# Second expert pass: activation loads on GpSimd's queue, gating in place, gate map built eight tokens at a time

## The chip, the cores and the metric

The kernel runs on one core of a Trainium2 chip. The metric is the time of one execution on the device in microseconds (us). Engines: TensorE (PE) multiplies matrices, VectorE (DVE) and ScalarE (ACT) work elementwise, GpSimd (POOL) and SyncE (SP) do little more here than start transfers. Every engine runs its own list of instructions in order. A transfer (DMA) is started by an instruction on one engine's queue, waits there for what it depends on, and is then moved by the 16 DMA engines that all queues share.

## What is computed

Two transformer blocks on 256 tokens of width 1024, in fp32. The second block has two layers, and each ends in a layer of 16384 experts:

```python
def peer(h, w_q, sub_keys, u_emb, v_emb):
...
    q = jnp.einsum('td,dhk->thk', x_t, w_q).reshape(T, PEER_HEADS, 2, PEER_HALF)
    s = jnp.einsum('thpk,hpnk->thpn', q, sub_keys).astype(jnp.float32)
    sv, si = lax.top_k(s, K)
...
    fv, fpos = lax.top_k(cand, K)
...
    gate = jax.nn.softmax(fv, axis=-1)
    u = u_emb[eidx]
    v = v_emb[eidx]
    act = jax.nn.gelu(jnp.einsum('thkd,td->thk', u, x_t).astype(jnp.float32), approximate=False)
    return jnp.einsum('thk,thkd->td', (gate * act).astype(x_t.dtype), v)
```

Each token has 8 heads that choose 16 experts each; an expert has a row of `u` and a row of `v`.

## The kernel before

The kernel doesn't gather rows. It computes the activation of every token with every expert, multiplies it by a gate map G that is zero where an expert was not chosen, and multiplies the result by all of `v`. fp32 operands are split into a high and a low part (`wh`, `wl`), and a product is made of three matmuls: high times high, high times low, low times high. A weight tile of 1 MB is 128 x 2048 and is split in four 128x512 pieces by `split_w` (L302 on ScalarE makes `wh`, L303 on VectorE makes `wl`).

`peer(l)` (L1369 to 1694) runs once in each layer:

- **Queries.** Eight `feat2` blocks give the scores; the top 16 of each are found on VectorE. Before that, `xd` is stored to DRAM (L1374), the only transfer that goes through GpSimd's queue.
- **First expert pass** (L1595 to 1609): 64 blocks over `peer_u`, each with one weight tile, matmuls L370 and L373, gelu, and a store of 256 KB of activations to DRAM on ScalarE's queue (L1604). Between the matmuls a list of side work is run at a set pace (`tick`, `side`): the selection, and then the gate map, four tokens at a time. `onehots` (L1530) makes two one-hot tables and a weighted one, with VectorE operations L1534 to L1536; `onelow` (L1539) makes the low part, L1541; `build` (L1543) multiplies them in eight f16 matmuls (L1547, L1548), which ScalarE copies into G (128 x 128 x 256 fp32). There are 64 such groups in a layer.
- **Second expert pass** (L1629 to 1641): for each of 64 steps `n`, a weight tile of `peer_v` (L1635, SyncE's queue, three buffers `w`), the gated activations from `gated(n)`, and 24 matmuls 128x512 (L423) into four accumulators.

`gated(n)` (L1577) loads 256 KB of activations `ag` (L1580, SyncE's queue), multiplies by G into `wt` (L1582, VectorE), and splits `wt` in high (L1589, ScalarE) and low (L1590, VectorE). `ag` and `wt` are tiles of the tag `k2`, which has five buffers of 128x512 fp32 (`NK2 = 5`) for all temporaries of the kernel. A load can start when a buffer of the tag is free.

During the second pass of layer 0 the kernel also loads 52 tiles of 512 KB of `ada_w` (L482, SyncE's queue) into parts of G that are used up, and VectorE reduces each (L483). In layer 1 that work is absent. The scheduler of the language fixes the order of each engine's instructions when the program is built.

`diag` (L209), a helper of the first block and the mixers, scales an identity matrix and has a tag of its own, `dg`, with two buffers.

Of the kernel before, what the change touches and what calls it, by code (L numbers as in the profile page):

```python
# [8 lines left out]
F32 = mybir.dt.float32  # L9
F32R = mybir.dt.float32r  # L10
F16 = mybir.dt.float16
# [8 lines left out]
P = 128  # L20
S = 256
# [10 lines left out]
NK2 = 5  # L32
# [43 lines left out]
def body(tc, A, out, dbg=None, stop=None):  # L76
    nc = tc.nc
    es = ExitStack()

    def pool(name, bufs=1, space=None, stack=es):  # L80
        kw = {} if space is None else {"space": space}
        return stack.enter_context(tc.tile_pool(name=name, bufs=bufs, **kw))
# [14 lines left out]
    st = pool("stage", 2)  # L97
# [110 lines left out]

    def diag(r):  # L209

        d = st.tile([P, P], F32, name="dg", bufs=2)
        nc.vector.tensor_scalar(d, ident, r, None, op0=OP.mult)
        return d

# [315 lines left out]
    def row_of(i, r):  # L530

        pr = pmm.tile([P, 512], F32, name="mm")
        for t in range(2):
            nc.tensor.matmul(pr[:, t * P:(t + 1) * P], ones, diag(r[:, t:t + 1]), start=True, stop=True)
        nc.scalar.activation(rows_rms[:, i, :], pr[:, 0:S], AF.Copy)
# [404 lines left out]
    for t in range(2):  # L940
        nc.tensor.matmul(pr[:, t * P:(t + 1) * P], ones, diag(rf[:, t:t + 1]), start=True, stop=True)
# [46 lines left out]
    for t in range(2):  # L988
        a_, b_ = ssx[:, 2 * t:2 * t + 1], ssx[:, 2 * t + 1:2 * t + 2]
        e_, c_ = r2_[:, 2 * t:2 * t + 1], r2_[:, 2 * t + 1:2 * t + 2]  # L990
        nc.vector.tensor_scalar(e_, a_, b_, D * EPS, op0=OP.add, op1=OP.add)
        nc.vector.tensor_scalar(e_, e_, EPS, None, op0=OP.mult)
        inv_rms(c_, ssf[:, 2 * t:2 * t + 1], ssf[:, 2 * t + 1:2 * t + 2], e_)
        by0.append(diag(c_))
# [374 lines left out]
    def peer(l, x, by, xstack):  # L1369
# [10 lines left out]
        ip = pool("peeri", stack=ps0)  # L1380
# [48 lines left out]
        def add(cost, f, *a):  # L1429
            side.append((cost, lambda: f(*a)))  # L1430
# [68 lines left out]
        def select():  # L1499

            for t in range(2):
                add(0.75, pairs, t)
                for h in range(8):
                    add(0.65, top16, FV[:, t, h], FP[:, t, h], cand[:, t, h])
                add(0.5, tables, t)
                add(0.8, places, t)
            add(1.4, gates)
            for t in range(2):
                wc = [(w, c) for w in range(2) for c in range(0, 16, 4)]
                for n, (w, c) in enumerate(wc):  # L1510
                    add(0.78, terms, t, w, c)
                    if n:
                        add(0.0, entry, t, *wc[n - 1])
                add(0.0, entry, t, *wc[-1])
                add(0.6, slots, t)
# [4 lines left out]
        def over(w, t0):  # L1520


            return ijg[:, w, t0:t0 + 4, None, :].to_broadcast(four)

        def pairs_of(v):
            return v.rearrange("p t (j a) -> p t j a", a=2)
# [3 lines left out]
        def onehots(t0):  # L1530
            ab = st.tile([P, 2, 4, P], F16, name="k2", bufs=NK2)
            a, b = ab[:, 0], ab[:, 1]
            e = ip.tile([P, 4, P], F16, name="ohe", bufs=2)
            nc.vector.tensor_tensor(pairs_of(e), places2, over(1, t0), op=OP.is_equal)  # L1534
            nc.vector.tensor_tensor(pairs_of(a), places2, over(0, t0), op=OP.is_equal)
            nc.vector.tensor_mul(pairs_of(b), pairs_of(e), over(2, t0))  # L1536
            hot[t0] = a, b, e
# [28 lines left out]
        side.popleft()[1]()  # L1566
        select()
        add(0.0, gate_map)
        for t0 in range(0, S + 8, 4):
            if t0 < S:  # L1570
                add(1.0, onehots, t0)
            if 4 <= t0 < S + 4:
                add(0.35, onelow, t0 - 4)
            if t0 >= 8:
                add(0.0, build, t0 - 8)

        def gated(n):  # L1577

            ag = st.tile([P, 2, S], F32, name="k2", bufs=NK2)
            nc.sync.dma_start(ag.rearrange("p j t -> p (j t)"), actd[n])  # L1580
            wt = st.tile([P, 2, S], F32, name="k2", bufs=NK2)
            nc.vector.scalar_tensor_tensor(wt, ag, 1.0 / GATE, G[0][:, 2 * n:2 * n + 2, :], op0=OP.mult, op1=OP.mult)  # L1582
            if n:
                whl = q4.tile([P, 2, 2, S], F32R, name="q4")
                wh_, wl_ = whl[:, 0], whl[:, 1]
            else:
                wh_ = st.tile([P, 2, S], F32R, name="k2", bufs=NK2)
                wl_ = st.tile([P, 2, S], F32R, name="k2", bufs=NK2)
            nc.scalar.activation(wh_, wt, AF.Copy)  # L1589
            nc.vector.tensor_sub(wl_, wt, wh_.bitcast(F32))  # L1590
            return wh_, wl_


        actd = []
        pace["rate"] = sum(c for c, _ in side) / (4 * 56)  # L1595
        for g in range(64):
            def ev_act(acc):
                ag = st.tile([P, 2, S], F32, name="k2", bufs=NK2)
                if g < LATE:
                    both(ag, acc)  # L1600
                    acc = ag
                nc.scalar.activation(ag, acc, AF.Gelu)
                ad = dr.tile([P, 2 * S], F32, name=f"act{l}_{g}")
                nc.scalar.dma_start(ad, ag.rearrange("p j t -> p (j t)"))  # L1604
                actd.append(ad)
            (feat2 if g < LATE else feat)(hl, A["peer_u_2"], (l * 64 + g) * P * 2048, ev_act)
            if g == 61:
                side_done()
                first_w = gated(0)
# [19 lines left out]
        for n in range(64):  # L1629
# [4 lines left out]
            w = wp.tile([P, 2048], F32, name="w")  # L1634
            nc.sync.dma_start(w, dap(A["peer_v_2"], l * 16384 * 1024 + n * 2048, [[P * 1024, P], [1, 2048]]))  # L1635
            wh_, wl_ = first_w if n == 0 else gated(n)
            if n < 63:
                for i in range(2):
# [35 lines left out]
    if stop == "xm0":  # L1674
        b1.close(); es.close()
        return
    x, ss, xs_ = peer(0, x, by, b1)
    dump("xp0", x)
    if stop == "xp0":
# [4 lines left out]
    if stop == "xm1":  # L1684
        xs_.close(); es.close()
        return
    x, ss, xs_, frow = peer(1, x, by, xs_)
    r_ = nrm.tile([P, 2], F32, name="rx2")
    o = out.rearrange("(t p) d -> p t d", p=P)
# [144 lines left out]
```

## Time and profile before

| | us |
|---|---|
| runs shown | 2221.74, 2221.75, 2216.76 |
| median | 2221.74 |
| profiled execution | 2223.68 |
| its span | 2221.9 |
| first expert pass, layers 0 and 1 | 523.9 to 897, 1477.8 to 1862 |
| second expert pass, layers 0 and 1 | 907.5 to 1264.6, 1861.6 to 2205.5 |

In the second pass the matmuls of line 423 begin and end the stage; the times in the last row are the starts of the first and the last of them. The span runs from the first to the last instruction of the profiled execution; the rest of its time lies around it. The granted clock of TensorE was 1.00 of full in every stretch shown. In views of the trace, `L1582 DVE` is an instruction of line 1582 on VectorE, `k<-k,G` are the tiles it writes and reads, and `[0.49 <-DMA k<-act]` says that its engine had been idle for 0.49 us before it and what ended that.

### The profile page before, as it was taken

What the parts mean: (1) busy time and instruction counts of PE and PEld (TensorE: products, weight loads), DVE (VectorE), ACT (ScalarE), POOL (GpSimd) and SP (SyncE); (2) the same over time, 40 slices, a digit from 0 to 9 for tenths busy, and PEclk for the clock granted to TensorE, in tenths of its full rate; (3) what the DMA queues carried; (4) which work ended last, traced back from release to release, by engine and by line L of the source; (5) the groups of instructions that cost most, each with busy time, mean ns of one, the idle gap of its engine ahead of it and who ended that gap; (6) DMA issues with size and microseconds to landing.
All of it is one profiled execution on the core that took longest, in us unless ns stands there. A gap on an engine that the chain in (4) does not pass through costs nothing.

```text
span 2221.9 us, 36167 instructions
## 1 busy us (share of the span) xinstructions
PE 2183.6 (98%) x12792; PEld 1865.7 (84%) x12792; DVE 1826.7 (82%) x4379; ACT 1326.6 (60%) x2448; POOL 21.2 (1%) x28
## 2 busy tenths in 40 slices
PE   8999999999999999999999999999999999999998
PEld 7889998888888888878777787888888888888886
DVE  7778888689988887688888888899888876777776
ACT  7656555555666666555555566566666666555554
POOL 0000000000000000000000010000000000000000
PEclk9999999999999999999999999999999999999999
DMA  6246787445655555889999643456555557666663
GB/s 244 96 167 256 271 303 281 160 173 206 226 212 207 198 212 209 283 314 332 323 321 322 215 157 122 171 193 239 203 201 210 196 212 259 250 248 245 244 240 143
DMA packets 107286, 503.30 MB, mean 227 GB/s; under 512 B 12513, under 2 KB 13665, under 8 KB 61794
## 3 DMA queue, kind: packets, MB, share of 16 engines
q1 hardware_dynamic: 87954, 465.19, 58.4%
q10 hardware_dynamic: 18864, 33.72, 4.1%
q8 instruction: 100, 1.64, 0.3%
q0 software_dynamic: 288, 2.10, 0.2%
q14 instruction: 80, 0.66, 0.1%
HBM read 464.25 MB, written 36.70 MB: 225 GB/s over the span
## 4 chain that ended last, share of the span: by engine, by line
PE 84%; DVE 7%; DMA 6%; ACT 1%; issue 1%; SPq 0%; DVEq 0%; ACTq 0%
PE acc L373 24%; PE acc L423 22%; PE acc L370 12%; DMA k<-act 6%; PE acc L308 4%; PE acc L311 4%; PE acc L312 4%; DVE wl L303 3%; PE acc L320 3%; PE acc L321 3%; PE acc L319 3%; PE mm L1547 1%; PE mm L1548 1%; DVE G L483 1%; PE pt L267 1%
## 5 line engine op out<-in xcount | busy, mean ns | idle before, releaser
L302 ACT ACTIVATE wh<-w 128x512 fp32r<-128x512 f32 (+1 forms) x1408 | 879.6, 630 | 652.6 <-PE acc L423 247.5
L303 DVE TENSOR_TENSOR wl<-w,wh 128x512 fp32r<-128x512 f32 (+1 forms) x1408 | 951.9, 689 | 205.7 <-ACT wh L302 198.2
L373 PE MATMUL acc<-q,wh 128*128 128x512 f32 x2240 | 797.3, 402 | 0.0
L423 PE MATMUL acc<-wh,q 128*128 128x512 f32 x1984 | 611.0, 390 | 0.0
L370 PE MATMUL acc<-q,wl 128*128 128x256 f32 x2240 | 584.3, 281 | 1.0 <-DVE wl L303 1.0
L373 PEld LDWEIGHTS acc<-q,wh 128*128 128x128 f32 x2240 | 408.1, 188 | 69.9
L370 PEld LDWEIGHTS acc<-q,wl 128*128 128x128 f32 x2240 | 422.6, 189 | 22.7 <-DVE wl L303 2.1
L423 PEld LDWEIGHTS acc<-wh,q 128*128 128x128 f32 x1984 | 372.4, 188 | 76.7
L423 PE MATMUL acc<-wl,q 128*128 128x512 f32 x992 | 387.4, 392 | 7.3 <-DVE wl L303 7.0
L423 PEld LDWEIGHTS acc<-wl,q 128*128 128x128 f32 x992 | 186.2, 188 | 52.7 <-DVE wl L303 14.5
L1582 DVE SCALAR_TENSOR_TENSOR k<-k,G 128x512 f32<-128x512 f32 x128 | 88.2, 690 | 65.9 <-DMA k<-act 65.0
L1410 ACT ACTIVATE k<-acc 128x512 f32<-128x512 f32 x124 | 74.0, 597 | 96.9 <-PE acc L373 96.8
L320 PE MATMUL acc<-q,wh 128*128 128x256 f32 x416 | 117.8, 284 | 0.5 <-DVE q L245 0.5
L319 PE MATMUL acc<-q,wh 128*128 128x256 f32 x416 | 117.3, 283 | 0.7 <-ACT q L244 0.7
L321 PE MATMUL acc<-q,wl 128*128 128x256 f32 x416 | 117.5, 283 | 0.0
L1411 DVE TENSOR_TENSOR k<-acc,k 128x512 f32<-128x512 f32 x124 | 85.0, 686 | 17.6 <-ACT k L1410 17.3
L311 PE MATMUL acc<-wl,q 128*128 128x512 f32 (+1 forms) x224 | 89.4, 400 | 0.0
L1590 DVE TENSOR_TENSOR q<-k,q 128x512 fp32r<-128x512 f32 x126 | 86.2, 684 | 0.8
L312 PE MATMUL acc<-wh,q 128*128 128x512 f32 (+1 forms) x224 | 86.6, 400 | 0.0
L308 PE MATMUL acc<-wh,q 128*128 128x512 f32 (+1 forms) x224 | 85.9, 402 | 0.4 <-ACT q L244 0.4
L1589 ACT ACTIVATE q<-k 128x512 fp32r<-128x512 f32 x126 | 77.8, 617 | 13.8 <-DVE k L1582 13.8
L320 PEld LDWEIGHTS acc<-q,wh 128*128 128x128 f32 x416 | 79.7, 192 | 0.8 <-DVE q L245 0.7
(459 smaller groups left out, 2660.4 us busy)
## 6 DMA issues: line engine op xcount, KB each, us to landing
w<-in_peer_u_dram SPq DMA_DIRECT2D x128, 1024.0 KB, 4.9
w<-in_peer_v_dram SPq DMA_DIRECT2D x128, 1024.0 KB, 5.3
act<-k ACTq DMA_DIRECT2D x128, 256.0 KB, 3.0
k<-act SPq DMA_DIRECT2D x128, 256.0 KB, 5.4
G<-in_ada_w_dram SPq DMA_DIRECT2D x52, 512.0 KB, 7.2
w<-in_w_gu_dram SPq DMA_DIRECT2D x22, 1024.0 KB, 4.8
adw<-in_ada_w_dram SPq DMA_DIRECT2D x44, 512.0 KB, 5.6
w<-in_peer_w_q_dram SPq DMA_DIRECT2D x16, 1024.0 KB, 4.9
```

The costliest lines, as they stand in the source:

```text
L302: ada_p["act"] = nc.scalar.activation(h[:, :n], src, AF.Copy).ins.name
L303: i_ = nc.vector.tensor_sub(l[:, :n], src, h[:, :n].bitcast(F32))
L308: i_ = nc.tensor.matmul(ps, lh, wh, start=start, stop=False)
L311: nc.tensor.matmul(ps, lh, wl, start=False, stop=False)
L312: i_ = nc.tensor.matmul(ps, ll, wh, start=False, stop=stop)
L319: nc.tensor.matmul(ps, wh, h, start=start, stop=False)
L320: nc.tensor.matmul(ps, wh, l, start=False, stop=False)
L321: nc.tensor.matmul(ps, wl, h, start=False, stop=stop)
L370: nc.tensor.matmul(to[:, 0, :], wl[:, ws], part(hl, k, 0), start=False, stop=False)
L373: nc.tensor.matmul(to.rearrange("p a s -> p (a s)"), wh[:, ws], hl[k // 2][:, k % 2].rearrange("p a s -> p (a s)"), start=k == 0, stop=k == 7)
L423: nc.tensor.matmul(ps[t, hf], lhs, ww[hf], start=first and lhs is h and ww is wh, stop=last and lhs is l)
L1582: nc.vector.scalar_tensor_tensor(wt, ag, 1.0 / GATE, G[0][:, 2 * n:2 * n + 2, :], op0=OP.mult, op1=OP.mult)
```

## The change

Four edits. The load of the activations moves from SyncE's queue to GpSimd's, and their product with G overwrites them, so that `gated` takes one buffer of `k2` where it took two. In the gate map, two groups of four tokens are built one right after the other, `onelow` follows its own `onehots`, and the tag `ohe` has three buffers. `diag` takes a buffer of `k2` where it had a tag of its own. Lines behind the edit move down by three: L1580, L1582, L1589, L1590 and L1635 are L1583, L1585, L1592, L1593 and L1638 after the change.

```diff
--- before.py
+++ after.py
@@ -208,7 +208,7 @@
 
     def diag(r):
 
-        d = st.tile([P, P], F32, name="dg", bufs=2)
+        d = st.tile([P, 512], F32, name="k2", bufs=NK2)[:, 0:P]
         nc.vector.tensor_scalar(d, ident, r, None, op0=OP.mult)
         return d
 
@@ -1530,7 +1530,7 @@
         def onehots(t0):
             ab = st.tile([P, 2, 4, P], F16, name="k2", bufs=NK2)
             a, b = ab[:, 0], ab[:, 1]
-            e = ip.tile([P, 4, P], F16, name="ohe", bufs=2)
+            e = ip.tile([P, 4, P], F16, name="ohe", bufs=3)
             nc.vector.tensor_tensor(pairs_of(e), places2, over(1, t0), op=OP.is_equal)
             nc.vector.tensor_tensor(pairs_of(a), places2, over(0, t0), op=OP.is_equal)
             nc.vector.tensor_mul(pairs_of(b), pairs_of(e), over(2, t0))
@@ -1566,19 +1566,22 @@
         side.popleft()[1]()
         select()
         add(0.0, gate_map)
+
         for t0 in range(0, S + 8, 4):
             if t0 < S:
                 add(1.0, onehots, t0)
-            if 4 <= t0 < S + 4:
-                add(0.35, onelow, t0 - 4)
-            if t0 >= 8:
+            if t0 >= 8 and t0 % 8 == 0:
                 add(0.0, build, t0 - 8)
+                add(0.0, build, t0 - 4)
+            if t0 < S:
+                add(0.35, onelow, t0)
 
         def gated(n):
 
             ag = st.tile([P, 2, S], F32, name="k2", bufs=NK2)
-            nc.sync.dma_start(ag.rearrange("p j t -> p (j t)"), actd[n])
-            wt = st.tile([P, 2, S], F32, name="k2", bufs=NK2)
+
+            nc.gpsimd.dma_start(ag.rearrange("p j t -> p (j t)"), actd[n])
+            wt = ag
             nc.vector.scalar_tensor_tensor(wt, ag, 1.0 / GATE, G[0][:, 2 * n:2 * n + 2, :], op0=OP.mult, op1=OP.mult)
             if n:
                 whl = q4.tile([P, 2, 2, S], F32R, name="q4")
```

The number of instructions stays the same on PE, DVE and ACT. The 128 loads of activations leave SyncE's list and stand in GpSimd's, in the order of `n`.

**VectorE in the second pass of layer 1.** `k_23128` and `k_23130` are one step's `ag` and `wt`, and the numbers of the next step are higher by 49. Before:

```order
L1590 TENSOR_TENSOR q_22936<-k_22934,q_22936 128x512
L1582 SCALAR_TENSOR_TENSOR k_23130<-k_23128,G 128x512
L303 TENSOR_TENSOR wl<-w,wh 128x512 x4
L1590 TENSOR_TENSOR q_22985<-k_22983,q_22985 128x512
L303 TENSOR_TENSOR wl<-w,wh 128x512
L1582 SCALAR_TENSOR_TENSOR k_23179<-k_23177,G 128x512
L303 TENSOR_TENSOR wl<-w,wh 128x512 x3
L1590 TENSOR_TENSOR q_23034<-k_23032,q_23034 128x512
```

After the change a step has one buffer, and numbers rise by 48:

```order
L1593 TENSOR_TENSOR q_22846<-k_22843,q_22846 128x512
L303 TENSOR_TENSOR wl<-w,wh 128x512 x3
L1585 SCALAR_TENSOR_TENSOR k_23083<-k_23083,G 128x512
L303 TENSOR_TENSOR wl<-w,wh 128x512
L1593 TENSOR_TENSOR q_22894<-k_22891,q_22894 128x512
L303 TENSOR_TENSOR wl<-w,wh 128x512 x3
L1585 SCALAR_TENSOR_TENSOR k_23131<-k_23131,G 128x512
L303 TENSOR_TENSOR wl<-w,wh 128x512
L1593 TENSOR_TENSOR q_22942<-k_22939,q_22942 128x512
```

Between `L1593` of a step and the multiplication five steps later, which takes the same buffer (`k_22843`, then `k_23083`), stand three `L303`, or two in every fourth step; right behind the multiplication come one or two `L303` and the next `L1593`.

**VectorE in the second pass of layer 0.** Before:

```order
L1582 SCALAR_TENSOR_TENSOR k_11902<-k_11900,G 128x512
L303 TENSOR_TENSOR wl<-w,wh 128x512
L1590 TENSOR_TENSOR q_11802<-k_11800,q_11802 128x512
L488 TENSOR_TENSOR mod<-mod,cols 128x8
L303 TENSOR_TENSOR wl<-w,wh 128x512 x3
L483 SCALAR_TENSOR_TENSOR G,mod<-G 128x1024
L1582 SCALAR_TENSOR_TENSOR k_11953<-k_11951,G 128x512
L303 TENSOR_TENSOR wl<-w,wh 128x512
```

After, with the numbers rising by 50 or 51 a step:

```order
L1593 TENSOR_TENSOR q_11837<-k_11834,q_11837 128x512
L1585 SCALAR_TENSOR_TENSOR k_12034<-k_12034,G 128x512
L303 TENSOR_TENSOR wl<-w,wh 128x512 x3
L483 SCALAR_TENSOR_TENSOR G,mod<-G 128x1024
L303 TENSOR_TENSOR wl<-w,wh 128x512
L1593 TENSOR_TENSOR q_11887<-k_11884,q_11887 128x512
L1585 SCALAR_TENSOR_TENSOR k_12085<-k_12085,G 128x512
```

Here the multiplication that takes the buffer of `k_11834` is that of `k_12085`; a whole step of VectorE's work stands between the `L1593` that frees the buffer and it.

## Rows read from the trace of the kernel before

**Rows 1.** Windows: length, busy us (and count) by engine, PE clock, DMA share, GB/s.

```profile
523.86:897.00 373.14, 372.65 (x2489) 320.31 (x2488) 322.70 (x832) 245.96 (x426) 0.00 (x0) 1.00 0.60 213
943.00:1247.00 304.00, 296.73 (x1290) 239.86 (x1289) 259.36 (x443) 164.78 (x270) 0.00 (x0) 1.00 0.89 318
1900.00:2202.00 302.00, 302.00 (x1338) 250.15 (x1337) 217.22 (x338) 168.05 (x276) 0.00 (x0) 1.00 0.66 238
```

**Rows 2.** The same for line 423 alone, both second expert passes.

```profile
907.50:1264.55 357.05, 349.77 (x1511) 281.45 (x1512) 1.00 0.86 308
1861.60:2205.50 343.90, 343.89 (x1511) 283.34 (x1512) 1.00 0.67 240
```

**Rows 3.** Waits (us, times, longest): 907 to 1262, 943 to 1247, 1900 to 2202.

```profile
PE acc L423 <- DVE wl L303: 7.0, 11, 1.1
...
DVE k L1582 <- DMA k<-act: 44.3, 42, 2.6
...
DVE k L1582 <- DMA k<-act: 14.0, 11, 3.1
```

**Rows 4.** DMA issues, count, KB, median us to landing: 943 to 1247, 1862 to 2200.

```profile
k<-act SPq DMA_DIRECT2D x54, 256.0 KB, 6.7
...
k<-act SPq DMA_DIRECT2D x62, 256.0 KB, 3.2
```

**Rows 5.** Timeline, layer 0: start, us, engine, line; VectorE, then SyncE's queue.

```profile
1030.74 0.69 DVE L1582 SCALAR_TENSOR_TENSOR k<-k,G 128x512 f32<-128x512 f32 x1 [1.33 <-DMA k<-act]
...
1034.90 0.68 DVE L1590 TENSOR_TENSOR q<-k,q 128x512 fp32r<-128x512 f32 x1
1035.74 0.69 DVE L1582 SCALAR_TENSOR_TENSOR k<-k,G 128x512 f32<-128x512 f32 x1 [0.15 <-DMA k<-act]
...
1041.08 0.69 DVE L1582 SCALAR_TENSOR_TENSOR k<-k,G 128x512 f32<-128x512 f32 x1 [0.49 <-DMA k<-act]
...
1035.62 0.36 SPq L1580 DMA_DIRECT2D k<-act  x1
```

**Rows 6.** Timeline, layer 1: VectorE, then SyncE's queue.

```profile
2005.31 0.69 DVE L1582 SCALAR_TENSOR_TENSOR k<-k,G 128x512 f32<-128x512 f32 x1
...
2010.78 0.69 DVE L303 TENSOR_TENSOR wl<-w,wh 128x512 fp32r<-128x512 f32 x1
2011.39 0.68 DVE L1582 SCALAR_TENSOR_TENSOR k<-k,G 128x512 f32<-128x512 f32 x1
...
2006.03 0.32 SPq L1580 DMA_DIRECT2D k<-act  x1
```

**Rows 7.** GpSimd's two transfers (line 1374), and SyncE's load of the same tensor.

```profile
L1374 POOL DMA_DIRECT2D xd<-xf x1: 702/702/702, 450.5 to 450.5; - x1
...
DMA to landing us min/median/max: 5.7/6.3/6.9
...
w<-xd SPq DMA_DIRECT2D x2, 1024.0 KB, 4.7
```

**Rows 8.** Timeline of TensorE around one build in layer 0's first pass.

```profile
699.73 0.28 PE L370 MATMUL acc<-q,wl 128*128 128x256 f32 x1
...
700.09 0.28 PE L370 MATMUL acc<-q,wl 128*128 128x256 f32 x1
700.21 0.23 PE L1547 MATMUL mm<-k 128*128 128x128 f16 x1
...
700.55 0.22 PE L1547 MATMUL mm<-k 128*128 128x128 f16 x1
...
700.95 0.28 PE L370 MATMUL acc<-q,wl 128*128 128x256 f32 x1
```

**Rows 9.** Groups of VectorE, 523.86 to 897: count, busy, mean ns, idle before.

```profile
L1534 DVE TENSOR_TENSOR ohe<-iota,ijg 128x512 f16<-128x512 f16 x64 | 27.1, 424 | 15.2 <-PE mm L1548 14.6
L1541 DVE TENSOR_TENSOR ohe<-ohe,ijg 128x512 f16<-128x512 f16 x64 | 26.9, 421 | 0.9
L1536 DVE TENSOR_TENSOR k<-ohe,ijg 128x512 f16<-128x512 f16 x64 | 26.7, 418 | 0.2
```

## The prediction

> **What bounds the kernel now.** I read the windows first, since a stage shows its limit there. In the first expert pass of layer 0 TensorE is busy for 372.65 of 373.14 us, and in the second pass of layer 1 for 302.00 of 302.00 us [rows 1]. Both are at TensorE's pace, and nothing that another engine does faster can shorten them. The second pass of layer 0 is the exception: 296.73 of 304.00 us, with the DMA engines at 0.89 and VectorE busy for 259.36 us [rows 1]. The two second passes do the same 1512 matmuls, and the windows of line 423 alone show 357.05 us for layer 0 and 343.90 us for layer 1 [rows 2]. So layer 0 loses 13.1 us, and the ideal step is 343.9 / 63 = 5.46 us, call it 5.45.
>
> Who is late there? The list of waits says that TensorE waited for `wl`, 7.0 us in 11 waits, and that VectorE, which makes `wl`, waited 44.3 us in 42 waits for the loads of activations [rows 3]. Those take 6.7 us from issue to landing in layer 0, and 3.2 us in layer 1 [rows 4]. The timeline shows one: it is issued at 1035.62, as L1590 of an earlier step has freed a buffer (1034.90 + 0.68), and the multiplication waits until 1041.08 [rows 5]. In layer 1 a load goes out at 2006.03, as the multiplication of 2005.31 ends, and the next multiplication is at 2011.39, behind other work [rows 6]: 5.36 us are there for a load of 3.2 us. That is the slack which layer 1 has and layer 0 hasn't.
>
> **The change, part by part.**
>
> *Layer 0, second pass.* Gating in place doesn't bring the loads forward by as much as two buffers saved would suggest: the scheduler runs the multiplication farther ahead, and all five buffers are held until `L1593` of a step has read them. The load of step n+5 leaves at the end of `L1593` of n. In the rows after the change, one step of VectorE's work stands between that instruction and the multiplication that needs the load. Follow the load, its multiplication, and VectorE's work up to the next but one `L1593`: that is one latency L, 0.04 us to issue (1035.62 against 1035.58, [rows 5]) and one step of work, 1030.74 to 1035.58 = 4.84 us [rows 5], for two steps. The step takes (L + 4.9) / 2, and TensorE's 5.45 us are met up to L = 6.0 us. What will L be? GpSimd's queue isn't shown with a load. Its two stores of 1 MB landed 5.7 and 6.9 us after issue; SyncE's loads of the same tensor took 4.7 us [rows 7]. So GpSimd's queue cost 1.0 to 2.2 us more. The least for L is layer 1's 3.2 + 1.0 = 4.2 us, and the stage then loses nothing (gain 13.1 us). The most is 6.7 + 2.2 = 8.9 us, a step of 6.9 us and a loss of some 1.45 x 50 steps = 73 us, less the 13.1 that are lost already: +59 us. I take L near the low end, since these loads no longer stand in a queue behind a weight tile and an `ada_w` tile; with the engines busy at 0.89 a little stays: **-10 us**.
>
> *Layer 1, second pass.* Here the new order costs. Between `L1593` of n and the multiplication of n+5 stand three `L303`, which come at TensorE's pace, and right behind the multiplication one `L303` and `L1593` of n+1, which frees the next buffer. The loop now closes within one step: issue 0.04, L, the multiplication (0.61 from start to next start, as 2010.78 to 2011.39, [rows 6]), on average 1.25 `L303` of 0.61, and 0.68 for `L1593` [rows 5]. A step takes L + 2.1 us, and TensorE's pace is met up to L = 3.35 us. The slack falls from 5.36 to 3.35 us while the load moves to the slower queue. SyncE's 3.2 us would still pass, and GpSimd's 4.2 (3.2 + 1.0) would not: 6.3 us a step, 0.85 too many over the 59 steps that have to wait for a buffer: **+50 us**. With the other measured surplus, L = 5.4, it is 7.5 us, or +121 us; the lower bound is 0, if L stays below 3.35. I take the lower surplus, because those stores moved four times the bytes, and part of their excess can be in moving.
>
> The Trainium skill, "DMA: Bandwidth & Descriptors", section "Anatomy of one DMA — SWDGE (gpsimd) path", gives for a transfer on this queue a fit of 2.0 us plus the bytes over 436e3 per us, 2.6 us for 256 KB as an estimate. By it layer 1 would lose nothing. The rows of the 1 MB stores speak against it: the fit gives 4.4 us as an estimate for those, and they took 5.7 and 6.9.
>
> *Gate map.* The eight f16 matmuls of a build are 0.057 us apart (700.21 to 700.55 for six), 0.45 us in all. From 700.09 to 700.95 pass 0.86 us where a pair of fp32 matmuls takes 0.36 (699.73 to 700.09) [rows 8]. What is left, 0.05 us, is the price of entering and leaving the f16 stretch. In TensorE's order the entries fall from 90 to 66 a layer, 48 in both, in a stage at TensorE's pace: **-2.6 us** (bounds 0 and -2.6: no row shows that the next build's cost shrinks too). The idle 14.6 us of VectorE before L1534 in layer 0, which waits for a free `ohe` [rows 9], goes with the third buffer, but hides under TensorE anyway.
>
> *In place, and `diag`.* An operation that overwrites its input is in the trace: L1541 takes 421 ns, and L1536, which doesn't, 418 [rows 9]. I take 0. `diag` in the shared tag moves nothing in any engine's order in the first block: 0, with 1 us each way. The 128 issues that leave SyncE shorten a queue that waits for buffers, not for time: 0.
>
> *The sum.* -10 + 50 - 2.6 = +37.4. The profiled execution of before took 2223.7 us, so 2261; it stands 1.9 above the median of the runs shown, which I take off: **2259 us**.
>
> **The rivals.**
>
> *Rival 1, faster: GpSimd's load is quick enough.* If L in layer 1 is at most 3.35 us, there's no new wait, and layer 0 gives back 10 to 13 us, the gate map up to 2.6: 2221.7 - 13 to 16, **about 2208 us**. For it: GpSimd's two stores ran beside another weight load on SyncE's queue, so part of the 1.0 to 2.2 us may be sharing; and the skill's fit stands on this side. Against it: in layer 1 the weight tile for a later step goes out within a step of every load too, so sharing isn't absent there.
>
> *Rival 2, no change: the loss and the gain cancel.* With L between 3.5 and 3.65 the layer 1 loop costs 0.15 to 0.3 us a step, 9 to 18 us, against the 13: **about 2222 us**. It needs a narrow L, and nothing in the rows points to it.
>
> *Rival 3, the heavy end: weight tiles collide with the loads.* If the weight tile of the step begins to move while the load, starting late, still moves, L takes the upper surplus, 5.4: +121 - 13, **about 2330 us**. The load on SyncE's queue in layer 0 shows what sharing does: 6.7 against 3.2 us [rows 4]. It is my forecast's mechanism with the larger price, and the upper end of the range leans to it.
>
> **How the numbers follow.** Slower, my forecast with its heavy end: 0.51. It rests on two transfers of another size, which is why it gets no more. Rival 1: 0.36. Rival 2: 0.13. About 0.3%, 6.7 us, is what a measurement of this kernel can tell from no change. The range of 2205 to 2300 takes in rival 1, rival 2 and the forecast up to L = 4.9 (2.1 + 4.9 - 5.45 = 1.55, x 59 = 91, less 12.6: +79); above it I leave some 0.15, below it 0.05. As cases of both signs hold much of the chance: the forecast's own range is 2229 to 2300.
>
> **What would show it.** In the profile after: the second pass of layer 0 at TensorE's pace, some 344 to 348 us, and its waits of VectorE for `act` nearly gone. In layer 1, line 1585 waiting for `k<-act` in most of the 64 steps, about 0.85 us each or more, TensorE waiting for `wl` by as much, and the loads' median there above 3.35 us; the weight loads unchanged. The gate map's stage shorter by 1 to 2 us a layer. The prediction is wrong if the median of these loads in layer 1 lies at or below 3.3 us: then the stage takes 344 us again. It is wrong in its mechanism if layer 1 loses time and line 1585 doesn't wait, or if layer 0 doesn't gain though its loads land within 6 us.

## The result, and the profile after

The changed kernel is slower: 2242.84 us (median, 2241.32 to 2248.26) against 2221.74, a ratio of 1.0101 with a 95% interval of 1.0075 to 1.0127. Its profiled execution took 2241.43 us, with a span of 2239.5 us, 17.6 more than before.

The windows of line 423 alone, over the two second expert passes of the changed kernel, answer to [rows 2] (length, TensorE's busy time and its matmuls, its weight loads, granted clock, DMA share, GB/s):

```profile
904.70:1255.30 350.60, 346.52 (x1512) 282.52 (x1512) 1.00 0.87 314
1856.30:2222.50 366.20, 353.39 (x1511) 283.32 (x1512) 0.99 0.65 225
```

Layer 0 went from 357.05 to 350.60 us and gained 6.5. Layer 1 went from 343.90 to 366.20 us and lost 22.3. The rest of the span is 1.8 us: the second pass of layer 0 begins 2.8 us earlier than before, the stretch between the two passes is 4.0 us longer, and what lies behind the second is 0.6 us longer. In that stretch TensorE's granted clock was 0.93 from 1255 to 1281 and 0.95 from 1345 to 1372, where the same work had 1.00 before; late2_sp below, whose second passes lose nothing, has 3.6 of these 4.0 us too, so they are no part of what is explained here.

The waits, of VectorE from 904 to 1257 and from 1856 to 2222, then of TensorE and of GpSimd in the latter stretch, answer to [rows 3]:

```profile
DVE k L1585 <- DMA k<-act: 42.1, 43, 2.9
...
DVE k L1585 <- DMA k<-act: 115.5, 55, 5.5
...
PE acc L423 <- DVE wl L303: 10.5, 12, 3.4
...
POOL k L1583 <- DVE q L1593: 282.0, 57, 7.2
```

In layer 1 VectorE waited 15.8 us in 14 waits for activations over the whole pass before ([rows 3] has a shorter stretch of it), and now 115.5 us in 55 of 64 steps. In layer 0 it waits nearly as much as before. TensorE, which had no wait in layer 1, now has 12 for `wl`, 10.5 us in all, the longest 3.4 us. Each load waits for the low split (L1593) that frees its buffer. The loads themselves, from 943 to 1240 and from 1856 to 2222, then the least, median and longest in 1880 to 2190, answer to [rows 4]:

```profile
k<-act POOLq DMA_DIRECT2D x49, 256.0 KB, 6.0
...
k<-act POOLq DMA_DIRECT2D x62, 256.0 KB, 3.0
...
DMA to landing us min/median/max: 2.7/3.0/5.5
```

So a load on GpSimd's queue has a median of 3.0 us in layer 1, less than the 3.2 us of before on SyncE's, and yet VectorE waits for it in nearly every step. The timeline shows a round of the loop (start, duration, engine and line; VectorE, then GpSimd):

```profile
1939.42 0.69 DVE L1585 SCALAR_TENSOR_TENSOR k<-k,G 128x512 f32<-128x512 f32 x1 [2.18 <-DMA k<-act]
1940.03 1.29 DVE L303 TENSOR_TENSOR wl<-w,wh 128x512 fp32r<-128x512 f32 x2
1941.23 0.68 DVE L1593 TENSOR_TENSOR q<-k,q 128x512 fp32r<-128x512 f32 x1
1941.83 1.89 DVE L303 TENSOR_TENSOR wl<-w,wh 128x512 fp32r<-128x512 f32 x3
1946.34 0.69 DVE L1585 SCALAR_TENSOR_TENSOR k<-k,G 128x512 f32<-128x512 f32 x1 [2.61 <-DMA k<-act]
1946.94 0.68 DVE L303 TENSOR_TENSOR wl<-w,wh 128x512 fp32r<-128x512 f32 x1
1947.55 0.69 DVE L1593 TENSOR_TENSOR q<-k,q 128x512 fp32r<-128x512 f32 x1
...
1942.21 0.55 POOL L1583 DMA_DIRECT2D k<-act  x1 [5.34 <-DVE q L1593]
1948.53 0.55 POOL L1583 DMA_DIRECT2D k<-act  x1 [5.77 <-DVE q L1593]
```

The low split ends at 1941.91, the load that it frees starts 0.30 us later on GpSimd, and the multiplication that waits for it starts at 1946.34. Behind it come one `L303` and the next low split, which frees the next buffer: from one load to the next it is 6.32 us, where TensorE needs 5.45. The load in this round took 4.0 us; with one of 3.0 us the same round would take 5.3 us and lose nothing. So the median doesn't tell the loss, but the mean does: the mean of the 53 loads is 3.4 us. Over the 52 steps from 1880 to 2190 the multiplication started 3.82 us on average after the low split that frees its buffer, and VectorE's work from there to the next low split's end is 2.05 us (0.61 + 1.25 x 0.61 + 0.68). That makes 5.87 us a step, and from one low split to the next the trace has 5.87 us on average. Before, a load was due a whole step after its issue [rows 6].

### The profile page after: what moved, and what is told of

It is laid out like the page before. It is cut to its first block, busy times and chain, and to the rows that moved or that the text cites. A ratio compares the mean times of both kernels' runs of the same rounds, so it can differ in the third digit from the quotient of the medians.

```text
span 2239.5 us, 36276 instructions
## 1 busy us (share of the span) xinstructions
PE 2190.0 (98%) x12792; PEld 1870.5 (84%) x12792; DVE 1809.4 (81%) x4379; ACT 1327.6 (59%) x2448; POOL 91.5 (4%) x156
## 4 chain that ended last, share of the span: by engine, by line
PE 67%; issue 24%; DVE 3%; POOL 3%; DMA 2%; ACT 1%; POOLq 0%; DVEq 0%; SPq 0%; ACTq 0%
PE acc L373 23%; PE acc L370 12%; PE acc L423 5%; PE acc L308 4%; PE acc L311 4%; PE acc L312 4%; POOL k L1583 3%; PE acc L320 3%; PE acc L321 3%; PE acc L319 3%; PE mm L1547 1%; PE mm L1548 1%; DMA k<-act 1%; DVE wl L303 1%; PE pt L267 1%
## 5 line engine op out<-in xcount | busy, mean ns | idle before, releaser
L303 DVE TENSOR_TENSOR wl<-w,wh 128x512 fp32r<-128x512 f32 (+1 forms) x1408 | 942.2, 688 | 172.5 <-ACT wh L302 167.2
L373 PE MATMUL acc<-q,wh 128*128 128x512 f32 x2240 | 788.7, 401 | 0.0
L423 PE MATMUL acc<-wh,q 128*128 128x512 f32 x1984 | 613.2, 391 | 3.1 <-ACT q L1592 3.1
L373 PEld LDWEIGHTS acc<-q,wh 128*128 128x128 f32 x2240 | 406.2, 188 | 71.8
L423 PEld LDWEIGHTS acc<-wh,q 128*128 128x128 f32 x1984 | 373.6, 188 | 80.9 <-ACT q L1592 3.9
L423 PE MATMUL acc<-wl,q 128*128 128x512 f32 x992 | 389.9, 395 | 13.8 <-DVE wl L303 12.9
L423 PEld LDWEIGHTS acc<-wl,q 128*128 128x128 f32 x992 | 186.9, 188 | 64.4 <-DVE wl L303 26.3
L1585 DVE SCALAR_TENSOR_TENSOR k<-k,G 128x512 f32<-128x512 f32 x128 | 88.4, 692 | 158.0 <-DMA k<-act 157.6
L1583 POOL DMA_DIRECT2D k<-act x128 | 70.0, 547 | 1482.5 <-PE acc L373 856.5
L1593 DVE TENSOR_TENSOR q<-k,q 128x512 fp32r<-128x512 f32 x126 | 86.4, 686 | 0.1
L1592 ACT ACTIVATE q<-k 128x512 fp32r<-128x512 f32 x126 | 77.7, 616 | 8.8 <-DVE k L1585 8.8
```

Source lines behind the costliest of these rows:

```text
L303: i_ = nc.vector.tensor_sub(l[:, :n], src, h[:, :n].bitcast(F32))
L373: nc.tensor.matmul(to.rearrange("p a s -> p (a s)"), wh[:, ws], hl[k // 2][:, k % 2].rearrange("p a s -> p (a s)"), start=k == 0, stop=k == 7)
L423: nc.tensor.matmul(ps[t, hf], lhs, ww[hf], start=first and lhs is h and ww is wh, stop=last and lhs is l)
L1583: nc.gpsimd.dma_start(ag.rearrange("p j t -> p (j t)"), actd[n])
```

## The experiments

Three theories stood. **Theory 1:** with one buffer a step, the scheduler puts the multiplication of step n+5 close behind the low split of n that frees its buffer, with at most three `L303` between, and the loop of load, multiplication and low split closes within one step. **Theory 2:** GpSimd's queue is the cost, by its own latency or by what it does to the weight loads. **Theory 3:** the gate map's edits upset the second pass, or the shared tag does.

| run | us, median | ratio to before, interval | second pass, layer 0 | layer 1 |
|---|---|---|---|---|
| changed kernel | 2242.84 | 1.0101, 1.0075 to 1.0127 | 350.6 | 366.2 |
| late2 | 2216.01 | 0.9971, 0.9962 to 0.9981 | 346.1 | 345.8 |
| sp_inplace | 2244.10 | 1.0101, 1.0084 to 1.0117 | 348.6 | 366.4 |
| late2_sp | 2212.38 | 0.9954, 0.9937 to 0.9971 | 344.3 | 344.1 |
| map_only | 2221.85 | 0.9999, 0.9988 to 1.0009 | 360.1 | 344.0 |
| pool_only | 2214.32 | 0.9968, 0.9954 to 0.9981 | 345.6 | 345.8 |
| late4 | 2223.33 | 1.0006, 0.9993 to 1.0020 | 351.7 | 345.5 |
| no_map | 2239.70 | 1.0084, 1.0065 to 1.0104 | 350.5 | 363.4 |
| inplace_only | 2239.85 | 1.0077, 1.0054 to 1.0100 | 351.4 | 362.3 |
| min_fix | 2214.07 | 0.9964, 0.9953 to 0.9974 | 344.4 | 344.0 |
| few_weights | 2215.97 (one run) | | 348.2 | 343.4 |

The two last columns are the lengths of line 423's windows in each profile. For layer 0 one profile is a rough measure: VectorE has the same order there in few_weights as in the changed kernel, and the lengths are 348.2 and 350.6 us. The medians of before in the three sets of runs were 2222.58, 2221.54 and 2222.01 us.

**The multiplication later (late2).** The edit ties VectorE's order alone; `follow` ties two instructions' order without a semaphore. The orders of GpSimd and SyncE stay; in the traces 173 of TensorE's 12792 matmuls and 13 of ScalarE's 2579 instructions stand in another place than in the changed kernel.

```diff
-            nc.vector.scalar_tensor_tensor(wt, ag, 1.0 / GATE, G[0][:, 2 * n:2 * n + 2, :], op0=OP.mult, op1=OP.mult)
+            m_ = nc.vector.scalar_tensor_tensor(wt, ag, 1.0 / GATE, G[0][:, 2 * n:2 * n + 2, :], op0=OP.mult, op1=OP.mult)
...
-            nc.vector.tensor_sub(wl_, wt, wh_.bitcast(F32))
+            if n >= 3:
+                follow(m_, lows[n - 2])
+            lows[n] = nc.vector.tensor_sub(wl_, wt, wh_.bitcast(F32)).ins.name
```

> The changed kernel, with one thing more: VectorE's multiplication of step n may not stand before the low split of step n-2 in its order, so that a load has three steps from its issue to its use where the changed kernel has most of one. Buffers, queue and all else as in the changed kernel. Theory 1 (the loop of load, multiplication and low split closes within one step, and GpSimd's load just doesn't fit): second pass of layer 1 back to 344 to 347 us from 366.2, layer 0 at 344 to 348 us from 350.5, in all 2210 to 2218 us. Theory 2 (GpSimd's queue itself is the cost, its loads or what they do to the weight loads): layer 1 stays above 358 us, in all above 2232 us.

Measured: 345.8 us in layer 1 and 2216.01 us in all, as theory 1 had it. The waits of VectorE and of TensorE in layer 1, and the loads from 1856 to 2200, of this kernel:

```profile
DVE k L1587 <- DMA k<-act: 1.8, 2, 1.5
...
PE acc L423 <- ACT q L1594: 1.5, 1, 1.5
...
k<-act POOLq DMA_DIRECT2D x61, 256.0 KB, 3.7
```

The loads take longer than in the changed kernel (3.7 against 3.0 us) and nobody waits: 115.5 us of waits have become 1.8. What decides is whether the load fits in the time that the order leaves for it, not how long it takes by itself.

**SyncE's queue with all else changed (sp_inplace).** The one line of the load goes back to `nc.sync`.

> The changed kernel with the load of activations back on SyncE's queue; in place, gate map and the order of VectorE as in the changed kernel. Theory 1: the time from the low split to the multiplication is 0.04 + 3.2 us for a load that meets nothing else, just under the 3.35 us that the loop allows, and more when it meets a weight tile; layer 1 still loses, 350 to 362 us, and layer 0 is at 350 to 360 us, since the load stands behind a weight tile and an ada_w tile; in all 2225 to 2245 us. Theory 2: layer 1 at 344 us, in all 2215 to 2222 us.

Measured: 366.4 us in layer 1, slightly more than theory 1's 350 to 362, 348.6 us in layer 0, slightly less than its 350 to 360, and 2244.10 us, the same as the changed kernel. Theory 2 falls: the loss doesn't need GpSimd's queue. The first row is VectorE's wait in layer 1, the second the loads from 1880 to 2190, the third the loads in layer 0 from 940 to 1240:

```profile
DVE k L1585 <- DMA k<-act: 116.5, 56, 4.0
...
DMA to landing us min/median/max: 2.4/4.2/5.7
...
k<-act SPq DMA_DIRECT2D x50, 256.0 KB, 6.4
```

The scheduler's order isn't quite that of the changed kernel: two `L303` instead of three stand before the multiplication in every second step, where it was every fourth, so two come behind it as often. The sum closes here too: 3.65 us on average from the low split to the multiplication, and 0.61 + 1.5 x 0.61 + 0.68 us of VectorE's work, make 5.86 us a step, and the trace has 5.86. In layer 0 the loads take 6.4 us, against 6.0 us on GpSimd's queue in the changed kernel, and the pass isn't longer.

**Both together (late2_sp).**

> As the run with the later multiplication, with the load on SyncE's queue. Theory 1: with three steps for a load the queue doesn't matter, so within 4 us of that run, 2208 to 2218 us; layer 1 at 344 to 346 us. Theory 2: layer 1 at 344 us and faster than the GpSimd version by 15 us or more.

Measured: both passes at TensorE's pace, 344.3 and 344.1 us, and 2212.38 us, 10 us below the kernel before: the fastest version here. The stretch 1880 to 2190 of its loads:

```profile
DMA to landing us min/median/max: 3.4/4.0/5.3
```

No load is as quick as the median of the changed kernel, and the list of TensorE's waits in that pass is empty. Against late2 it is quicker by 3.6 us. 1.5 us in each pass is one wait at the start, `PE acc L423 <- ACT q L1594: 1.5, 1, 1.5` in late2 for the high part of an early step; late2_sp doesn't have it.

**The queue alone (pool_only).** The kernel before, with `nc.sync` replaced by `nc.gpsimd` in line 1580.

> The kernel before with the loads of activations on GpSimd's queue and nothing else changed: a buffer for the load and one for the product, so that a load is issued as the multiplication of one step ends and is due at the next, about 4.8 us in layer 1. Theory 1: 3.0 us of transfer and 0.3 of delay before it fit most of the time, layer 1 344 to 350 us; layer 0 at 348 to 356, since the load no longer stands behind a weight and an ada_w tile; in all 2213 to 2224 us. Theory 2 (the queue is the cost): layer 1 above 355 us, in all above 2230.

Measured: 2214.32 us, 7 us faster than before, layer 0 at 345.6 us, below the expected 348 to 356, and layer 1 at 345.8 us. The queue pays by itself in layer 0, where the loads take 5.3 us (median, 943 to 1240) against 6.7 before. How much of that is the place in the queue isn't shown, since the scheduler gave VectorE another order there as well (two `L303` on each side of the low split). In layer 1 VectorE waits for loads, `DVE k L1582 <- DMA k<-act: 59.2, 40, 3.4`, and TensorE loses nothing but the wait at the start.

**In place alone (inplace_only).** The kernel before with `wt = ag`.

> The kernel before with the product of activations and gate map in place and nothing else; loads on SyncE's queue, the scheduler's own order. Theory 1: the short loop comes with this edit alone, so layer 1 at 362 to 368 us and layer 0 at 347 to 352, as in the run with in place on SyncE's queue; in all 2236 to 2247 us. If the loss needs one of the other edits beside it, layer 1 is at 344 to 350 us and the kernel at 2222 us or less.

Measured: 362.3 us in layer 1, 351.4 in layer 0, 2239.85 us. This edit by itself brings the loss in layer 1, and by itself it shortens layer 0 by 5.7 us on SyncE's queue. With a buffer saved in each step the scheduler runs the multiplication farther ahead, and in layer 1 that leaves a load less time than before.

**The gate map: alone (map_only), and taken back (no_map).** `map_only` is the kernel before with the map's edits and that of `diag`. `no_map` is the changed kernel with the map as before.

> The kernel before with the edits of the gate map and of diag alone; loads on SyncE's queue into a buffer of their own, as before. Both theories: second passes as before (357 and 344 us); the first passes shorter by 0.3 us each, as the changed kernel's trace has it, or by 1.3 each as the prediction's price had it; in all 2218 to 2222 us, no change. If it is slower by more than 5 us, the shared tag k2 is to blame for a part of the loss.

> The changed kernel with the gate map built as before (four tokens, two buffers of ohe). Theory 1: the loss stays, layer 1 at 364 to 368 us, in all 2240 to 2246 us. Theory 3 (the gate map's new order or its third buffer upsets the second pass): 2225 us or less.

Measured: 0.9999 for the map alone, with an interval of 0.9988 to 1.0009 (its layer 0 is at 360.1 us, layer 1 at 344.0), and 2239.70 us without it, with 363.4 us in layer 1. These last two lie just under what theory 1 expected, and the loss is nearly whole. Theory 3 falls. Both versions without the map's edits stand 3 to 4 us below their partners with them (363.4 and 366.2 us in layer 1, 362.3 and 366.4). Their intervals overlap, so this difference isn't shown.

**The least shift (late4).** As late2, with `n - 4` in place of `n - 2`.

> The changed kernel with the least shift of the multiplication: not before the low split of step n-4, so one low split later than now. Theory 1: that one shift puts a whole step of VectorE's work between issue and use, so the loop runs over two steps and allows 8 us; layer 1 at 344 to 348 us, layer 0 at 344 to 350, in all 2212 to 2222 us. If more distance were needed (a load late by bursts, weight tiles that wait for each other), layer 1 would lose at least 5 us and lie between that of the changed kernel (366) and that of the run with n-2 (345.7).

Measured: layer 1 at 345.5 us, with one low split more between issue and use: a loop over two steps instead of one is enough, as theory 1 had it. Layer 0 is at 351.7 us, just outside the expected 350, since this order is there what the changed kernel has already. In all 2223.33 us, 1.3 above the upper end of what was expected, and no different from the kernel before. In its profile the two passes together are some 4 us shorter than before; why the medians don't show it is open.

**Few weight tiles (few_weights).**

```diff
+            if l == 0 or n < 3 or n == 63:
+                w = wp.tile([P, 2048], F32, name="w")
...
+                kept.append(w)
+            else:
+                w = kept[n % 3]
```

> The changed kernel, which in the second pass of layer 1 loads only the first three weight tiles and the last and multiplies with those throughout (the output is another). It tells whether weight tiles that move at the same time lengthen the loads of activations. If they do: nearly every load lands within 3.0 us of its start, 0.3 + 3.0 is within the 3.35 us of the loop, and layer 1 takes 344 to 350 us. If GpSimd's transfers are late by themselves, the spread of 2.9 to 5.4 us stays, and layer 1 takes 360 us or more.

Measured: layer 1 at 343.4 us, with the changed kernel's order of VectorE. The loads from 1880 to 2190 and VectorE's wait in that pass:

```profile
DMA to landing us min/median/max: 2.7/2.9/4.0
...
DVE k L1585 <- DMA k<-act: 51.0, 42, 2.9
```

In the changed kernel 20 of the 53 loads of that stretch took over 3.1 us, here 3 of 51. So GpSimd's transfer by itself fits in the loop, 0.30 + 2.9 against 3.35 us, and it is the weight tiles moving beside it that push the loop over TensorE's pace. The changed kernel loses only with both: the short loop (late2 takes it away) and the tiles beside it (few_weights does).

**The least repair (min_fix).** The kernel before with `wt = ag` and the order of late2.

> The kernel before with the product in place and the multiplication not before the low split of step n-2; loads on SyncE's queue, gate map and diag as before. Theory 1: both second passes at TensorE's pace, 344 to 346 us, in all 2208 to 2216 us, within 3 us of the run that has the map and diag edits too (2212.4). If those edits carried part of its gain, it lies above 2216 us.

Measured: 344.4 and 344.0 us, 2214.07 us in all, within 2 us of late2_sp. In place with the right order pays by itself; neither GpSimd's queue nor the map is needed for it.

## Why the prediction was right, and where its terms were off

- **What bounds the kernel** stood: the first passes at TensorE's pace, the second pass of layer 0 held by loads. All versions that repair the loads in both layers end at 344 to 346 us in both second passes.
- **Layer 0, -10 us:** it measured -6.5. The loop over two steps held: loads took 6.0 us (median), not near 4.2, and with the 0.30 us on GpSimd, 6.3 + 4.9 over two gives 5.6 us a step, slightly above TensorE's pace. The other half of the reason did not hold. The loads were to be quicker because they no longer stand behind a weight tile and an `ada_w` tile; put back there (sp_inplace) they take 6.4 us, and layer 0 is at 348.6 us.
- **Layer 1, +50 us:** the loop was right. The new order closes it within one step, and a step takes the time from the low split to the multiplication and 2.05 us more (5.87 us in both sum and trace). What the prediction put into it was wrong. L was put at 4.2 us, SyncE's 3.2 and a surplus of 1.0 us that GpSimd's queue had shown with 1 MB stores; 256 KB loads on that queue have a median of 3.0 us. Stores of 1 MB in the changed kernel still took 5.8 and 7.2 us, so the surplus belongs to those transfers and was no price for the small ones. Without the surplus the prediction's own sum has no loss: "SyncE's 3.2 us would still pass". It doesn't pass: in place on SyncE's queue layer 1 takes 366.4 us (sp_inplace) and 362.3 (inplace_only).
- **What made up the +22.3** is the long loads, which a median hides. Weight tiles lengthen 20 loads of 53, as few_weights shows, so that the mean is 3.4 us; GpSimd starts a load 0.30 us after the low split, where the sum had 0.04. From low split to multiplication 3.82 us were measured, 0.42 us a step too many, or some 25 us over 59 steps (an estimate). The sum had 4.24 us there. That it came so near is luck: the queue's surplus, which it added, wasn't there, and the weight tiles, which it left to rival 3, were. The right sign rests on the loop and on this luck.
- **TensorE's clock** is a small part. TensorE's listed waits are 12.0 of the 22.3 us (10.5 for `wl`, 1.5 at the start), and its matmuls are busy for 9.5 us longer (353.39 against 343.89). Some of that is clock: right after its longest wait, of 3.4 us, 14 matmuls took the 6 us of the window below at a granted clock of 0.50 (1.2 GHz), where 14 at 0.227 us (343.90 / 1512) would take 3.2. sp_inplace loses 22.5 us in layer 1 at a granted clock of 1.00 throughout.

```profile
2097.00:2103.00 6.00, 5.77 (x14) 4.50 (x15) 4.53 (x9) 1.26 (x2) 0.55 (x1) 0.50 0.54 169
```

- **The Trainium skill's fit of 2.0 us plus bytes** was weighed wrongly. The Trainium skill, "DMA: Bandwidth & Descriptors", section "Anatomy of one DMA — SWDGE (gpsimd) path", gave an estimate of 2.6 us for these loads; the trace has 2.7 at least and 2.9 (median) without weight tiles. The rows of the two stores, which I set against it, were of another size and direction. But by that estimate alone layer 1 would have lost nothing, and it lost 22.3 us: the load by itself isn't the whole loop.
- **The gate map, -2.6 us:** not shown. map_only gained nothing that its interval of 0.1% either way can tell from zero; a gain of 2.6 us would lie at the interval's very end. The price of entering an f16 stretch was worked out from one build; the fewer entries didn't show as time.
- **The signs that it named:** by one of them the step on L failed. It said that with a median at or below 3.3 us in layer 1 "the stage takes 344 us again"; the median is 3.0 and the stage takes 366.2, because the delay at the start and the longer loads count. Line 1585 waits in most steps of layer 1, as named. TensorE's waits for `wl` are 10.5 us there and not as much as VectorE's 115.5, VectorE's waits in layer 0 are not nearly gone (42.1 us), layer 0 is not at 344 to 348 us, and the gate map's stage is no shorter (373.3 us in layer 0, 373.14 before).
- **Rival 1** was right on the queue (pool_only gains 7 us) and wrong on the sign, because in place and queue came together. **Rival 3** named what lengthens the loads, the weight tiles, and put it too high: the mean rose to 3.4 us, not to 5.4.

## What to carry to other kernels

Count how long the order leaves a buffer's refill, from the instruction that frees it to the first that needs it, on the engine that does both; saving a buffer can cost time if the scheduler spends it on running the consumer ahead. Where such a loop closes within one step, look at the mean and the tail of the transfer and at the delay before it, not its median alone. One edge in the order, at the price of one wait of 1.5 us in each pass at most, moved both stages to the bound here, on either queue.

## What the runs showed of the hardware

In layer 1, loads of 256 KB through GpSimd's queue took 3.0 to 4.1 us (medians of the runs with weight tiles beside them, 2.7 at least), and through SyncE's 3.2 to 4.3 us (2.4 at least). The median moved more with the order than with the queue: with the same ties it is 3.7 us on GpSimd's (late2) and 4.0 on SyncE's (late2_sp). The prediction had held GpSimd's to be at least 1 us slower. GpSimd's start 0.30 us after what releases them, SyncE's 0.03 to 0.04 us after. Without weight tiles beside them 3 loads of 51 took over 3.1 us, with them 20 of 53. Why 1 MB stores on that queue take 5.7 to 7.2 us where SyncE's load of the same tensor takes 4.7 was not tried.
